# A transformer trunk on one core: where the sums of weight blocks stand, and when weight buffers are returned

## The chip, the core and the metric

The kernel runs on one core of a Trainium2 chip. The core has five engines that run side by side, each with its own stream of instructions: TensorE (PE in the profile; its weight loads are shown as PEld), VectorE (DVE), ScalarE (ACT), GpSimd (POOL) and SyncE (SP), which here only starts DMAs. Weights lie in the chip's main memory and are copied by DMA into on-chip buffers. Matmul results go to eight banks of a separate memory (tiles named `ps`), from which VectorE or ScalarE reads them out; this is called an evacuation below.

The metric is the time of the whole kernel on the device in microseconds (us), a median of runs. Lower is better.

## What is computed

Two requests (512 and 256 tokens, width 1024) go through two layers with shared weights. Each layer is a feed-forward block, a token mixer (a gated linear recurrence in layer 0, windowed attention in layer 1) and a second feed-forward block. The four feed-forward blocks take most of the time, and the change touches only their weights:

```python
def swiglu_ffn(x, w1, w2):
    gate, up = jnp.split(x @ w1, 2, axis=-1)
    return (jax.nn.silu(gate) * up) @ w2

x = x + 0.5 * swiglu_ffn(rmsnorm(x, norm_g[li, 0]), ffn_w1[li, 0], ffn_w2[li, 0])
```

`w1` is 1024 x 5632 and `w2` 2816 x 1024, all in float32.

## The kernel before

**Precision.** TensorE multiplies in a shorter format here (`fp32r`). To keep float32 accuracy each operand is split into a high part (a cast on ScalarE, line 199 for these weights) and a low part (the difference, on VectorE, line 200), and each product is three matmuls: high x high, high x low, low x high.

**Seven products for eight.** The feed-forward products are done as 2 x 2 blocks with a Strassen-like scheme: seven products `p1` to `p7` of sums of blocks replace the eight of the plain scheme. For the weights this means four blocks `a11`, `a12`, `a21`, `a22` and sums of them. They are made in place in the buffers into which the weights were loaded (`wr` in the profile, four of them):

- a DMA that accumulates, started by POOL (`into`, line 141), adds `a22` onto `a21`. This sum is the weight of `p5`;
- another such DMA adds `a11` onto a separately loaded tile `s3`. This is the weight of `p7`;
- `second` (line 205, VectorE) adds `a21` onto `a11`. This is the weight of `p6`;
- `fourth` (line 206, VectorE) adds `a11` onto `a12`. This is the weight of `p3`.

`p1`, `p2` and `p4` take `a11`, `a12` and `a22` as they are; so `second` must come after `a11` was split for `p1` and copied onto `s3`, and `fourth` after `a12` was split for `p2`.

**Two kinds of block.** An *up pair* (`up_pair`, line 424) makes one 128-wide block of `gate` and one of `up` for all tokens: seven products of 12 matmuls over 384 columns (line 414), in the order p1, p7, p2, p5, p4, p6, p3. Its weight blocks are 512 wide and the high and low part of one product share one buffer. Between the products stand the evacuations: lines 431, 433 and 435 on ScalarE, 437, 440, 441, 442, 444, 446 and 448 on VectorE. Line 437 reads the bank of `p5`, on which `p3` then accumulates. A *down block* (`down_quad`) multiplies what four up pairs made by 512 rows of `w2`: seven products of 18 matmuls over 512 columns (line 472), in the order p1, p2, p5, p4, p7, p6, p3, each evacuated by three additions to `x` (line 494). `p2` accumulates on the banks of `p1`, `p4` on those of `p5`, `p3` on those of `p7`. Its weight blocks are 1024 wide, and a product takes two buffers. There are 80 up pairs and 20 down blocks, in groups of four pairs (in a feed-forward's first group two, after other work) and one down block.

After an up pair its two results are split and summed too (lines 259 and 260 for the splits, 343 to 347 for the sums), which gives the operands of the down block.

**Staging.** The split weights live in a ring of eight buffers (`w`). `done` returns the buffers of a product and calls `ahead`, which stages the next products as far as the ring allows; each staging step is one call of `step`, so one product. When all steps of a block have been called, the next block's loads can be issued by SP (line 151; the loads of `s3` are on line 185); they wait until the `wr` buffers they go into have been read for the last time. In `up_pair`, `done` is called at the end of `product`, so ahead of the evacuation that follows it in the code.

**What sets the order.** Each engine runs its instructions in a fixed order, and an instruction that waits holds those behind it on its engine. That order is not the order of the code: the framework places every instruction by its own estimate of when its inputs are there, and where several could go, the one that the code calls first. `issue_after(i)` adds an edge to that: what is traced in it on the engine of instruction `i` is placed behind `i`. It is an order, not a wait for `i` to finish.

Of the kernel before, what the change touches and what calls it, by code (L numbers as in the profile page):

```python
# [9 lines left out]
F32 = mybir.dt.float32  # L10
# [37 lines left out]
class Trunk:  # L48
# [123 lines left out]
    def quad_steps(self, key, raws, srcs, order):  # L172
        nc = self.nc
        flat = lambda t: t.rearrange("p a b -> p (a b)")
        up = len(raws) == 2
        if up:
            a11, a12, a21, a22 = (flat(t[:, h : h + 4, :]) for t in raws for h in (0, 4))
            three = [srcs[1].rearrange("(k p) c -> p k c", p=P)[:, :4, :]]
        else:
            a11, a12, a21, a22 = (flat(t) for t in raws)  # L180
            three = [srcs[2][:, i : i + 1, :] for i in range(2)]
        s3 = []
        for i, src in enumerate(three):
            t = self.wp.tile([P, 512], F32, tag="s3", name=self.name("s3"), bufs=2)
            self.last_load = nc.sync.dma_start(t.rearrange("p (a b) -> p a b", a=src.shape[1]), src)
            self.into(t, a11[:, i * 512 : (i + 1) * 512])
            s3.append(t)
        self.into(a21, a22)

        def split(name, srcs, eng=None):  # L190
            if up:
                w = self.wtile()
                hi, lo = w[:, :512], w[:, 512:]
            else:
                hi, lo = self.wtile(), self.wtile()
            n = srcs[0].shape[-1]
            for i, src in enumerate(srcs):
                h, l = (t[:, i * n : (i + 1) * n] for t in (hi, lo))
                nc.scalar.copy(h, src)  # L199
                (eng or nc.vector).tensor_sub(l, src, h.bitcast(F32))  # L200
            view = lambda t: t.rearrange("p (a b) -> p a b", a=4 if up else 2)
            self.staged[(*key, name)] = (view(hi), view(lo), 1 if up else 2)

        own = {"p1": [a11], "p2": [a12], "p3": [a12], "p4": [a22], "p5": [a21], "p6": [a11], "p7": s3}
        second = lambda: nc.vector.tensor_add(a11, a11, a21)  # L205
        fourth = lambda: nc.vector.tensor_add(a12, a12, a11)  # L206
        after = {"p1": second, "p2": fourth} if up else {"p7": second, "p6": fourth}

        def step(name):
            split(name, own[name], nc.gpsimd if up and name == "p5" else None)  # L210
            if name in after:
                after[name]()

        return [(1 if up else 2, lambda name=name: step(name)) for name in order]

    def stage_next(self):
# [41 lines left out]
    def split(self, src, hi, lo):  # L258
        self.nc.scalar.copy(hi, src)  # L259
        self.nc.vector.tensor_sub(lo, src, hi.bitcast(F32))  # L260
# [148 lines left out]
    def product(self, key, name, src, ps, first, last):  # L409
        wh, wl = self.take((*key, name))  # L410
        for k in range(4):
            a, b = (wh[:, k, :], wl[:, k, :]), self.operand(src, k)
            for i, (x, y) in enumerate(((0, 0), (0, 1), (1, 0))):
                self.nc.tensor.matmul(  # L414
                    ps,
                    a[x],
                    b[y],
                    start=first and k == 0 and i == 0,
                    stop=k == 3 and i == 2,
                    skip_group_check=True,  # L420
                )
        self.done((*key, name))

    def up_pair(self, tag, j):
        nc = self.nc
        key = (tag, j)
        a, b, c, d = (self.ps(H) for _ in range(4))
        v, w, t = (self.tmp(H) for _ in range(3))
        p = lambda name, ps, first, last: self.product(key, name, FACTOR[name], ps, first, last)
        p("p1", a, True, False)  # L430
        nc.scalar.copy(v, a)
        p("p7", c, True, False)
        nc.scalar.copy(w, c)
        p("p2", a, False, True)
        nc.scalar.activation(a, a, AF.Silu)
        p("p5", d, True, False)
        nc.vector.tensor_sub(w, w, d)  # L437
        p("p4", c, False, True)
        p("p6", b, True, True)
        nc.vector.tensor_sub(v, v, b)  # L440
        nc.vector.tensor_sub(t, c, v)
        nc.vector.tensor_mul(t, t, a)  # L442
        yield t
        nc.vector.tensor_sub(w, w, v)
        p("p3", d, False, True)
        nc.vector.tensor_add(v, v, d)
        self.last_act = nc.scalar.activation(v, v, AF.Silu).ins
        self.last_dve = nc.vector.tensor_mul(w, v, w).ins
        yield w

    def down_quad(self, tag, g, hid):
# [823 lines left out]
```

## Time and profile before

| | |
|---|---|
| median of 3 runs | 2866.38 us (2860.94, 2866.38, 2866.47) |
| span of the profiled execution | 2863.4 us |
| mean granted TensorE clock | 0.997 |
| matmuls of up pairs (line 414) | 1174.0 us busy, 6720 |
| matmuls of down blocks (line 472) | 587.2 us busy, 2520 |
| lows of weight splits on VectorE (line 200) | 519.4 us busy, 640 |
| sums on VectorE (lines 205 and 206) | 160.6 us busy, 200 |

The span runs from the first to the last instruction of the profiled execution. The page gives no separate device time for that execution; its span lies within the range of the three runs.

A row such as `1306.90 1.22 DVE L205 ... [6.53 <-DMA wr<-wr]` in a timeline reads: it starts 1306.90 us after the span's start, takes 1.22 us, runs on VectorE, comes from line 205, and the engine was idle for 6.53 us before it, until a DMA into a `wr` buffer landed. In groups, the numbers behind the bar are busy time, mean ns of one, and the idle time of the engine just before them, with what ended it. The matmuls overlap, and their ends are modelled.

### The profile page before, as it was taken

Reading aid. Unit: us, or ns where it says so; the run is one execution under the profiler, and the core shown is the slowest. Engines: PE = TensorE matmul, PEld = TensorE weight load, DVE = VectorE, ACT = ScalarE, POOL = GpSimd, SP = SyncE. Lnnn points to the kernel's source line nnn. Section 1 sums busy time; section 2 is a strip of 40 time slices with the busy share of each in tenths; the row PEclk is TensorE's granted clock in tenths of the full one; section 3 lists DMA queues with packets and bytes.
Section 4 is the critical chain, followed back from the end, with each engine's and each line's share of the span. In section 5 each row is a group of like instructions: output and inputs, shape, how many; then the busy total and the mean of one; then the engine's idle time right before and its main releaser. Section 6 shows DMA issues by size and latency. Waiting matters only on the chain.

```text
span 2863.4 us, 40520 instructions
## 1 busy us (share of the span) xinstructions
PE 2800.4 (98%) x15225; PEld 2556.8 (89%) x15225; DVE 2198.4 (77%) x3846; ACT 1318.5 (46%) x2454; POOL 304.4 (11%) x306
## 2 busy tenths in 40 slices
PE   8999999999999999999999999999999899999998
PEld 8899998889899889988998998999887779988997
DVE  7788788477577658788878877887859978778877
ACT  7344443434344435444445543444457755434443
POOL 1111120000000001111110111111000001111110
PEclk9999999999999999999999999999999999999999
DMA  6555454311111233555444355445412113554443
GB/s 166 126 124 125 116 133 119 109 45 38 52 38 30 74 88 89 133 129 124 118 118 109 88 134 126 121 119 122 126 63 74 45 38 92 132 129 120 120 122 96
DMA packets 330101, 291.37 MB, mean 102 GB/s; under 512 B 11608, under 2 KB 257840, under 8 KB 329904
## 3 DMA queue, kind: packets, MB, share of 16 engines
q1 hardware_dynamic: 294064, 212.43, 25.2%
q0 software_dynamic: 31680, 62.93, 12.5%
q10 hardware_dynamic: 4160, 13.42, 1.3%
q8 instruction: 119, 1.95, 0.3%
q14 instruction: 78, 0.64, 0.1%
HBM read 216.39 MB, written 9.44 MB: 79 GB/s over the span
## 4 chain that ended last, share of the span: by engine, by line
PE 68%; DVE 21%; DMA 5%; issue 3%; ACT 3%; DVEq 0%; ACTq 0%; POOLq 0%; SPq 0%
PE ps L414 24%; PE ps L472 11%; PE ps L254 8%; PE ps L255 8%; PE ps L256 8%; DVE w L200 5%; DVE big L260 3%; PE ps L664 3%; DVE x L494 3%; DMA wr<-wr 3%; DMA wr<-in_ffn_w_dram 3%; DVE tA L347 1%; DVE wr L206 1%; PE ps L758 1%; PE ps L316 1%
## 5 line engine op out<-in xcount | busy, mean ns | idle before, releaser
L414 PE MATMUL ps<-big,w 128*128 128x384 f32 x6720 | 1174.0, 335 | 6.6 <-DVE tA L437 6.2
L414 PEld LDWEIGHTS ps<-big,w 128*128 128x128 f32 x6720 | 1166.0, 188 | 12.7 <-DVE tA L437 11.2
L199 ACT CAST w<-wr 128x512 fp32r<-128x512 f32 x600 | 415.9, 707 | 724.2 <-PE ps L414 317.0
L472 PE MATMUL ps<-w,big 128*128 128x512 f32 x2520 | 587.2, 392 | 17.3 <-DVE x L494 17.3
L472 PEld LDWEIGHTS ps<-w,big 128*128 128x128 f32 x2520 | 470.4, 188 | 129.2 <-DVE x L494 16.6
L200 DVE TENSOR_TENSOR w<-wr,w 128x512 fp32r<-128x512 f32 (+1 forms) x520 | 437.1, 851 | 95.8 <-ACT w L199 87.1
L494 DVE SCALAR_TENSOR_TENSOR x<-ps,x 128x512 f32<-128x512 f32 x468 | 305.9, 683 | 20.4 <-PE ps L472 10.2
L141 POOL DMA_DIRECT2D s<-wr x120 | 105.6, 880 | 1619.8 <-DMA wr<-in_ffn_w_dram 585.7
L254 PE MATMUL ps<-w,big 128*128 128x512 f32 x624 | 248.9, 399 | 0.2
L256 PE MATMUL ps<-w,big 128*128 128x512 f32 x624 | 244.9, 393 | 2.2 <-DVE big L323 1.3
L255 PE MATMUL ps<-w,big 128*128 128x512 f32 x624 | 244.2, 391 | 0.0
L259 ACT CAST big<-tA 128x384 fp32r<-128x384 f32 x296 | 147.9, 513 | 178.9 <-DVE tA L442 77.1
L254 PE MATMUL ps<-big,w 128*128 128x384 f32 (+2 forms) x640 | 220.8, 346 | 3.4 <-ACT big L259 2.0
L255 PE MATMUL ps<-big,w 128*128 128x384 f32 (+2 forms) x640 | 216.9, 339 | 0.7 <-DVE big L260 0.5
L256 PE MATMUL ps<-big,w 128*128 128x384 f32 (+2 forms) x640 | 215.7, 337 | 0.0
L167 DVE TENSOR_TENSOR w<-wr,w 128x1024 fp32r<-128x1024 f32 x92 | 111.4, 1221 | 81.0 <-ACT w L166 56.9
L260 DVE TENSOR_TENSOR big<-tA,big 128x384 fp32r<-128x384 f32 x296 | 167.4, 576 | 8.1 <-ACT big L259 4.9
L205 DVE TENSOR_TENSOR wr<-wr,wr 128x512 f32<-128x512 f32 (+1 forms) x100 | 79.4, 794 | 119.1 <-DMA wr<-wr 89.7
L141 POOL DMA_DIRECT2D wr<-wr x100 | 87.2, 872 | 687.6 <-DVE tA L343 321.4
L166 ACT CAST w<-wr 128x1024 fp32r<-128x1024 f32 x92 | 96.6, 1052 | 120.3 <-PE ps L255 99.4
L256 PEld LDWEIGHTS ps<-w,big 128*128 128x128 f32 x624 | 117.1, 188 | 28.2 <-DVE big L323 2.0
L254 PEld LDWEIGHTS ps<-w,big 128*128 128x128 f32 x624 | 117.4, 188 | 22.4 <-issue 0.6
(170 smaller groups left out, 3296.8 us busy)
## 6 DMA issues: line engine op xcount, KB each, us to landing
wr<-in_ffn_w_dram SPq DMA_DIRECT2D x264, 512.0 KB, 3.9
s<-in_ffn_w_dram SPq DMA_DIRECT2D x120, 256.0 KB, 3.0
s<-wr POOLq DMA_DIRECT2D x120, 256.0 KB, 4.0
wr<-wr POOLq DMA_DIRECT2D x80, 256.0 KB, 3.8
wr<-in_hg_w_in_dram SPq DMA_DIRECT2D x40, 512.0 KB, 3.7
wr<-wr POOLq DMA_DIRECT2D x20, 512.0 KB, 4.6
spill<-x ACTq DMA_DIRECT2D x12, 512.0 KB, 3.1
x<-spill ACTq DMA_DIRECT2D x12, 512.0 KB, 3.3
```

The source lines that it names most:

```text
L141: self.nc.gpsimd.dma_start(out, src, accum_op=ALU.add)
L167: self.nc.vector.tensor_sub(lo, raw, hi.bitcast(F32))
L199: nc.scalar.copy(h, src)
L200: (eng or nc.vector).tensor_sub(l, src, h.bitcast(F32))
L254: nc.tensor.matmul(out, a[0], b[0], start=first, stop=False)
L255: nc.tensor.matmul(out, a[0], b[1], start=False, stop=False)
L256: nc.tensor.matmul(out, a[1], b[0], start=False, stop=last)
L259: self.nc.scalar.copy(hi, src)
L260: self.nc.vector.tensor_sub(lo, src, hi.bitcast(F32))
L414: self.nc.tensor.matmul(ps, a[x], b[y], start=first and k == 0 and i == 0, stop=k == 3 and i == 2, skip_group_check=True,)
L472: nc.tensor.matmul(ps, a[x], w[y], start=name == chain and kp == 0 and q == 0, stop=kp == 1 and q == 2, skip_group_check=True,)
L494: self.nc.vector.scalar_tensor_tensor(x, ps, c, x, ALU.mult, ALU.add)
```

## The change

Each sum moves from behind the split of an earlier product to right in front of the split that reads it. `second` is now part of the step of `p6`, and `fourth` of the step of `p3`, for both kinds of block. Each sum is placed behind the last low part that VectorE made for the same block (for an up pair that of `p4` and that of `p6`; for a down block that of `p7` and that of `p6`).

In `up_pair` the buffers are returned behind the evacuations: those of p1, p7, p2 and p5 after the evacuation next to them, those of p4 and p6 together after line 442 (as numbered before), that of p3 at the very end. `product` no longer returns them. `down_quad` is not touched.

```diff
@@ in quad_steps
             for i, src in enumerate(srcs):
                 h, l = (t[:, i * n : (i + 1) * n] for t in (hi, lo))
                 nc.scalar.copy(h, src)
-                (eng or nc.vector).tensor_sub(l, src, h.bitcast(F32))
+                low = (eng or nc.vector).tensor_sub(l, src, h.bitcast(F32)).ins
             view = lambda t: t.rearrange("p (a b) -> p a b", a=4 if up else 2)
             self.staged[(*key, name)] = (view(hi), view(lo), 1 if up else 2)
+            return low
 
         own = {"p1": [a11], "p2": [a12], "p3": [a12], "p4": [a22], "p5": [a21], "p6": [a11], "p7": s3}
-        second = lambda: nc.vector.tensor_add(a11, a11, a21)
-        fourth = lambda: nc.vector.tensor_add(a12, a12, a11)
-        after = {"p1": second, "p2": fourth} if up else {"p7": second, "p6": fourth}
+        sums = {"p6": (a11, a21), "p3": (a12, a11)}
+        last = [None]
 
         def step(name):
-            split(name, own[name], nc.gpsimd if up and name == "p5" else None)
-            if name in after:
-                after[name]()
+            if name in sums:
+                into, term = sums[name]
+                with self.tc.issue_after(last[0]):
+                    nc.vector.tensor_add(into, into, term)
+            low = split(name, own[name], nc.gpsimd if up and name == "p5" else None)
+            if not (up and name == "p5"):
+                last[0] = low
@@ in product
-        self.done((*key, name))
@@ in up_pair
+        free = lambda *names: [self.done((*key, name)) for name in names]
         p("p1", a, True, False)
         nc.scalar.copy(v, a)
+        free("p1")
         p("p7", c, True, False)
         nc.scalar.copy(w, c)
+        free("p7")
         p("p2", a, False, True)
         nc.scalar.activation(a, a, AF.Silu)
+        free("p2")
         p("p5", d, True, False)
         nc.vector.tensor_sub(w, w, d)
+        free("p5")
         p("p4", c, False, True)
         p("p6", b, True, True)
         nc.vector.tensor_sub(v, v, b)
         nc.vector.tensor_sub(t, c, v)
         nc.vector.tensor_mul(t, t, a)
+        free("p4", "p6")
         yield t
         nc.vector.tensor_sub(w, w, v)
         p("p3", d, False, True)
         nc.vector.tensor_add(v, v, d)
         self.last_act = nc.scalar.activation(v, v, AF.Silu).ins
         self.last_dve = nc.vector.tensor_mul(w, v, w).ins
+        free("p3")
         yield w
```

## The prediction

> **What bounds the kernel now.** I read the page first, then the chain of work that ended last, then the waits and the groups by shape, and last the timeline of one block of the feed-forward part.
>
> ```profile
> span 2863.4 us, 40520 instructions
> PE 2800.4 (98%) x15225; PEld 2556.8 (89%) x15225; DVE 2198.4 (77%) x3846; ACT 1318.5 (46%) x2454; POOL 304.4 (11%) x306
> ```
>
> TensorE is busy for 98% of the span, so any gain has to come out of its gaps. The full pace of its matmuls is read from undisturbed stretches of the chain (start, duration, what):
>
> ```profile
> 54.81 27.06 PE ps L414 x156
> 1237.96 14.80 PE ps L472 x64
> ```
>
> That is 0.173 us for one matmul of an up product (L414) and 0.231 us for one of a down product (L472). Now the waits that reach TensorE in these lines, and one that does not name it (engine, line, releaser: us in total, times, longest):
>
> ```profile
> PE ps L472 <- DVE x L494: 17.3, 37, 0.5
> PE ps L414 <- DVE tA L437: 6.2, 8, 2.3
> PEld ps L414 <- DVE tA L437: 11.2, 15, 2.7
> DVE wr L205 <- DMA wr<-wr: 89.7, 15, 8.2
> ```
>
> L494 and L437 are evacuations on VectorE. L205 is the first of the two sums of weight blocks. By shape it looks like this:
>
> ```profile
> L205 DVE TENSOR_TENSOR wr<-wr,wr 128x1024 f32<-128x1024 f32 x20 | 24.5, 1226 | 118.6 <-DMA wr<-wr 89.7 <-issue 28.9
> L205 DVE TENSOR_TENSOR wr<-wr,wr 128x512 f32<-128x512 f32 x80 | 54.9, 686 | 0.6
> L206 DVE TENSOR_TENSOR wr<-wr,wr 128x1024 f32<-128x1024 f32 x20 | 24.4, 1218 | 0.0
> ```
>
> All of the idle time stands before the 20 sums of the down blocks (1024 wide): 118.6/20 = 5.9 us each. The 80 of the up pairs wait for nothing. So each of the 20 down blocks has one place where VectorE stands still, and I read one of them. TensorE:
>
> ```profile
> 1309.79 2.35 PE L414 MATMUL ps<-big,w 128*128 128x384 f32 x12 [0.83 <-DVE tA L437]
> 1311.97 4.28 PE L472 MATMUL ps<-w,big 128*128 128x512 f32 x18
> 1316.80 10.27 PE L472 MATMUL ps<-w,big 128*128 128x512 f32 x44 [0.55 <-DVE x L494]
> 1327.52 14.80 PE L472 MATMUL ps<-w,big 128*128 128x512 f32 x64 [0.45 <-DVE x L494]
> ```
>
> Three waits: before p3 of the last up pair, before p2 of the down block (it accumulates on p1's bank, which must be read out first), and before p4 (on p5's bank; 44 = 18 of p2, 18 of p5, and 8 of p7 put ahead of p4). A shown gap understates the loss: a matmul is drawn 0.334 us long but follows its neighbour by 0.173, so 0.16 us more are lost at each. VectorE in the same stretch:
>
> ```profile
> 1299.16 1.22 DVE L200 TENSOR_TENSOR w<-wr,w 128x1024 fp32r<-128x1024 f32 x1
> 1306.90 1.22 DVE L205 TENSOR_TENSOR wr<-wr,wr 128x1024 f32<-128x1024 f32 x1 [6.53 <-DMA wr<-wr]
> 1308.05 1.22 DVE L200 TENSOR_TENSOR w<-wr,w 128x1024 fp32r<-128x1024 f32 x1
> 1309.18 0.55 DVE L437 TENSOR_TENSOR tA<-tA,ps 128x384 f32<-128x384 f32 x1
> 1309.64 1.22 DVE L206 TENSOR_TENSOR wr<-wr,wr 128x1024 f32<-128x1024 f32 x1
> 1310.78 1.22 DVE L200 TENSOR_TENSOR w<-wr,w 128x1024 fp32r<-128x1024 f32 x1
> 1311.92 0.55 DVE L440 TENSOR_TENSOR tA<-tA,ps 128x384 f32<-128x384 f32 x1
> 1313.90 1.22 DVE L200 TENSOR_TENSOR w<-wr,w 128x1024 fp32r<-128x1024 f32 x1
> 1315.97 0.68 DVE L494 SCALAR_TENSOR_TENSOR x<-ps,x 128x512 f32<-128x512 f32 x1
> ```
>
> The lows of p1, p2, p5 and p4 are the four L200. In the code the sum L205 is called after p7's split; here it ran second, before p2's low, and held VectorE 6.5 us for the accumulating DMA into a21. L437 waited behind it: product p5 ended some 24 matmuls (4.2 us) and the lost 1.0 us before 1309.79, at 1304.6, and L437 began at 1309.18. Then VectorE works without a gap up to the first L494, 0.7 us too late for p2.
>
> **The change: the sums.** For a down block both sums leave this stretch; L205 must follow p7's low, L206 p6's. No wait on the DMA moves with L205: the cast of p5 reads the same a21 earlier.
>
> ```profile
> 1301.10 1.05 ACT L199 CAST w<-wr 128x1024 fp32r<-128x1024 f32 x1
> 1306.84 1.06 ACT L199 CAST w<-wr 128x1024 fp32r<-128x1024 f32 x1 [3.62 <-DMA wr<-wr]
> ```
>
> These are the casts of p2 and p5. ScalarE still waits for the DMA at p5's, as before; its evacuations of the pair stand ahead of it.
>
> First term, L437. Without the sum, p2's low follows its cast (1302.2 to 1303.4) and L437 runs at 1304.6, when p5 ends. The wait before p3 goes: 6.2 + 8 × 0.16 = 7.5 us, and the seven waits that only the weight loads show (15 less 8) at about 0.15 each, 1 us: **8.5 us**. In one block the wait was so long that more came behind it (timeline of TensorE, then engines in windows, with the granted clock after POOL):
>
> ```profile
> 1723.71 3.14 PE L414 MATMUL ps<-big,w 128*128 128x384 f32 x12 [2.33 <-DVE tA L437]
> 1725.00:1727.00 2.00, 2.00 (x8) 1.98 (x7) 1.97 (x4) 0.00 (x0) 0.00 (x0) 0.51 0.00 1
> 1727.00:1729.00 2.00, 2.00 (x7) 1.54 (x6) 2.00 (x4) 0.51 (x1) 0.00 (x0) 0.64 0.84 244
> ```
>
> Clocks of 0.51 and 0.64 over 2 us each lose 1.0 + 0.7 = **1.7 us**, which go with the wait. The Trainium skill, "TensorE: Matmul & The Clock Gate", section "Part 1: The HAM clock gate", has the clock fall after an idle window of about 3.4 us; by that a gap of 2.33 us would not cause it, and the sum would be smaller by this term. Here it fell behind a shorter gap, so I keep the term.
>
> Second term, p2. p5's low now ends at 1307.9 + 1.15 = 1309.05. Behind it, at the paces of the rows (start to start), come L440 to L442 (1313.90 − 1311.92 = 1.98) and p4's low, L260 and L446 (1315.97 − 1313.90 = 2.07): the first L494 starts at 1313.1 and ends at 1313.8. TensorE, 1.0 us earlier, begins p1 at 1311.0 and wants p2 at 1311.0 + 18 × 0.231 = 1315.1: 1.3 us of cover. All 37 waits come to 17.3 + 37 × 0.16 = 23.2 us; divided as 0.71 to 0.61 that is **12.5 us** for p2's, which go, and 10.7 us for p4's. In the block of 1723.71 the DMA came 1.5 us later, and some of p2's wait stays there.
>
> Third term, p4. Before, 10.81 us pass from the first L494 to p5's, and p6's low is in them:
>
> ```profile
> 1322.74 0.69 DVE L200 TENSOR_TENSOR w<-s,w 128x512 fp32r<-128x512 f32 x1
> 1325.64 1.22 DVE L200 TENSOR_TENSOR w<-wr,w 128x1024 fp32r<-128x1024 f32 x1
> 1326.78 1.88 DVE L494 SCALAR_TENSOR_TENSOR x<-ps,x 128x512 f32<-128x512 f32 x3
> 1321.88 1.05 ACT L199 CAST w<-wr 128x1024 fp32r<-128x1024 f32 x1
> ```
>
> The sum (1.15 us) now stands behind p7's last low (1322.74), and p6's cast (1321.88) must wait for it; p6's low should then fall behind p5's evacuation. One goes in and one out: p5's first L494 starts at 1313.1 + 10.8 = 1323.9 and ends at 1324.6. p4 is wanted at 1311.0 + 54 × 0.231 = 1323.5, or 8 matmuls later (1325.3) if p7's still stand ahead. So the wait is between 0 and 1.1 us, against 0.61: from 10.7 us gained to 20 × 0.5 = 10 us lost. I take two thirds of the gain, **7 us**, since the order with the 8 matmuls is the one in the trace. p6's and p3's weights come some 3 us later (sum, cast 1.05, low 1.14 twice), at 1331 at the latest; p6 begins at 1311.0 + 90 × 0.231 = 1331.8 and p3 four us on. Cover of 1 us at the least; beyond it the cost is one for one.
>
> **What is held longer.** L205 reads a21, so a21's raw buffer comes free after it, no longer after p5's low. SP loads the next pair's weights into that buffer:
>
> ```profile
> 1312.03 3.49 SPq L151 DMA_DIRECT2D wr<-in_ffn_w_dram  x2
> 1331.74 0.62 ACT L199 CAST w<-wr 128x512 fp32r<-128x512 f32 x1 [5.62 <-PE ps L472]
> wr<-in_ffn_w_dram SPq DMA_DIRECT2D x264, 512.0 KB, 3.9
> s<-in_ffn_w_dram SPq DMA_DIRECT2D x120, 256.0 KB, 3.0
> s<-wr POOLq DMA_DIRECT2D x120, 256.0 KB, 4.0
> ```
>
> The load went out at 1312.03, as p5's low ended (1310.78 + 1.22). It will go out at 1321 to 1324, and the second load, the s3 load and POOL's two accumulations queue behind it: 3.9, then 3.0 and 4.0 with under 2 us of issuing, so p7's s3 stands at 1337 at the latest. Its split takes 1.3 us more; TensorE wants that at 1327.52 + 14.80, less the 2.3 us gained in this block, plus p1's 2.1: 1342.1. Hidden with some 4 us; ScalarE and VectorE may stand 2 to 3 us at p7's split, which I put at **2 us lost** in all. L206 holds a11's buffer in the same way, for a load wanted a pair later.
>
> **Up pairs.** 160 sums move by four products and cost the same 0.69 us. a21's buffer comes free 0.7 us later, against a lead of some 8 products (8 × 12 × 0.173 = 16.6 us). Nothing.
>
> **Returning buffers behind the evacuations.** It adds no instruction. The cast no longer stands ahead of L431, L433, L435: those come 0.5 us sooner, the cast as much later. No wait of TensorE names these three, so nothing is gained, and 0.5 us is covered by the same 16.6 us. p4's buffer comes back with p6's, some 4 us later; still covered, and costing nothing until the lead is gone.
>
> **Sum.** 8.5 + 1.7 + 12.5 + 7 − 2 = 27.7 us, from a span of 2863.4 to 2835.7. The runs shown have a median of 2866.38, 3.0 us above this span (they reach from 2860.94 to 2866.47, so this profiled execution is an ordinary one). Against the median: 2838.7, say **2839 us**.
>
> **Rivals.**
>
> *Only the L437 wait goes.* The gaps before p2 and p4 are alike in nearly every block, 0.55 and 0.45, although L205 waited between 5 and 8.2 us. That speaks for a cause that does not hang on the sum: too few banks, or the evacuation being simply wanted at once. Against it: VectorE is without a gap for 9 us before the first L494, and 3.5 us of that leave. It gives 8.5 + 1.7 = 10 us: 2856. The Trainium skill, "Perfetto Trace Analysis", section "Optimization Strategy", reads a repeating gap on the saturated engine as a possible lack of SBUF or PSUM for the next tile; by that, this rival is the right one. In these rows the releaser of each gap is an evacuation, which fits either reading.
>
> *The order does not follow.* The edges bind only VectorE's sums; everything else is ordered by the scheduler's own estimate, which put L205 where the DMA was not done. It can do the same with another instruction (p5's low ahead of L437 would bring back a wait of 1307.9 + 1.2 − 1304.6 − 4.2, about 0.3 us in a block, and p2's with it), or p4's term turns to 10 us lost. Gains and losses within 6 us: 2862 to 2870, centre 2866.
>
> *Slower: the late buffer starves the next pair.* The place is p7 of the first pair after each of 20 down blocks; the point is L205 ending about 4 us later than my 1324. Two more puts and three more evacuations ahead of it would do that, as p7's lows are already drawn apart by them. 2.5 us beyond the point at 20 places is 50 us, less the 30 us gained above: 2886. For it: the load's start moves by 9 to 12 us. Against it: the 4 us left.
>
> **How the numbers follow.** My forecast 0.57 (its own range 2829 to 2850), only L437 0.18, no follow-through 0.12, starved pair 0.13. Faster by over 0.2% (5.7 us, about what a measurement of this kernel can tell from no change): 0.57 + 0.18 = 0.75; within it 0.12; slower 0.13. The range leaves out the starved pair and a little below the forecast: 2828 to 2868.
>
> **What would show it.** Right: L205 of 1024 elements no longer has a DMA as releaser, stands behind p7's second low, and its 118.6 us of idle time are gone; PE L414 has no wait on L437; the L472 waits on L494 fall from 37 to under 15; no clock under 1 near the down blocks. Wrong: waits of L472 on L494 as many as before (second rival); waits of L414 on a cast or low of L199/L200 behind the down blocks (the starved pair); or VectorE idle before an L200 with a DMA or L199 as releaser while L437 is due.

## The result, and the profile after

The changed kernel takes 2833.75 us (median of 4 runs, 2833.56 to 2837.87) against 2866.28 us before: a ratio of 0.9897, 95% interval 0.9884 to 0.9910, so 32.5 us or 1.1% faster. The forecast was 2839 us. The profiled execution took 2833.56 us; its span is 31.6 us shorter than before:

```profile
span 2831.8 us, 40534 instructions
PE 2790.5 (99%) x15225; PEld 2559.2 (90%) x15225; DVE 2203.1 (78%) x3846; ACT 1320.2 (47%) x2453; POOL 307.3 (11%) x306
PE 91%; DVE 6%; ACT 2%; issue 1%; DMA 0%; DVEq 0%; ACTq 0%; SPq 0%
```

The third line is the chain of work that ended last. Before, TensorE held 68% of it, VectorE 21% and DMAs 5%; now TensorE holds 91%.

Line numbers have moved: up matmuls are L418 (were L414), down matmuls L482 (L472), both sums L213 (L205, L206), the evacuations of a down block L504 (L494), of p5 in an up pair L444 (L437), the copy of p1's bank L435 (L431). In the groups by shape (two rows of the kernel before, then the changed kernel), and then in the waits of the changed kernel:

```profile
L414 PE MATMUL ps<-big,w 128*128 128x384 f32 x6720 | 1174.0, 335 | 6.6 <-DVE tA L437 6.2
L472 PE MATMUL ps<-w,big 128*128 128x512 f32 x2520 | 587.2, 392 | 17.3 <-DVE x L494 17.3
```

```profile
L418 PE MATMUL ps<-big,w 128*128 128x384 f32 x6720 | 1173.8, 335 | 1.5 <-ACT tA L435 1.4
L482 PE MATMUL ps<-w,big 128*128 128x512 f32 x2520 | 576.6, 390 | 0.7 <-DVE x L504 0.6
L213 DVE TENSOR_TENSOR wr<-wr,wr 128x1024 f32<-128x1024 f32 x40 | 48.6, 1215 | 0.0
```

```profile
PEld ps L418 <- ACT tA L435: 6.4, 19, 0.8
PE ps L482 <- DVE x L504: 0.6, 1, 0.6
ACT w L199 <- DVE wr L213: 342.8, 132, 4.9
```

Busy plus idle time tells where the gain is. Before, the down matmuls had 587.2 + 17.3 = 604.5 us, now 576.6 + 0.7 = 577.3: 27.2 us gained. The up matmuls had 1174.0 + 6.6 = 1180.6, now 1175.3: 5.3 us. Together 32.5, which is the whole difference of the spans but for 0.9 us lost elsewhere. The 118.6 us for which VectorE stood before the wide sums are gone. Of the waits on L494 one is left, of 37; there is none on L444. One is new: TensorE's weight loads wait for the copy L435, and behind it is the third line: ScalarE now waits 342.8 us in all for sums of VectorE.

A down block of the changed kernel has no gap (timeline of TensorE, then of VectorE):

```profile
1304.59 28.92 PE L482 MATMUL ps<-w,big 128*128 128x512 f32 x126
```

```profile
1298.55 0.56 DVE L444 TENSOR_TENSOR tA<-tA,ps 128x384 f32<-128x384 f32 x1 [0.45 <-PE ps L418]
1302.08 1.23 DVE L200 TENSOR_TENSOR w<-wr,w 128x1024 fp32r<-128x1024 f32 x1 [2.98 <-ACT w L199]
...
1307.74 0.68 DVE L504 SCALAR_TENSOR_TENSOR x<-ps,x 128x512 f32<-128x512 f32 x1
...
1316.83 1.22 DVE L213 TENSOR_TENSOR wr<-wr,wr 128x1024 f32<-128x1024 f32 x1
...
1320.96 1.21 DVE L213 TENSOR_TENSOR wr<-wr,wr 128x1024 f32<-128x1024 f32 x1
```

```profile
1300.99 1.05 ACT L199 CAST w<-wr 128x1024 fp32r<-128x1024 f32 x1 [4.06 <-DMA wr<-wr]
```

L444, the evacuation of p5, runs as soon as p5 ends. The last row is ScalarE's cast of p5, which waits for the DMA; VectorE waits for that cast at p5's low (1302.08). The sums come 12 and 16 us after p1's start. But the cover before p2 is thin: p2 is due at 1304.59 + 18 × 0.231 = 1308.75, and p1's first evacuation ends at 1308.42.

### The profile page after: what moved, and what is told of

Same layout as the page of the kernel before. It is cut to its first block, busy times and chain, and to the rows that moved or that the text cites. A ratio compares the mean times of both kernels' runs of the same rounds, so it can differ in the third digit from the quotient of the medians.

```text
span 2831.8 us, 40534 instructions
## 1 busy us (share of the span) xinstructions
PE 2790.5 (99%) x15225; PEld 2559.2 (90%) x15225; DVE 2203.1 (78%) x3846; ACT 1320.2 (47%) x2453; POOL 307.3 (11%) x306
## 4 chain that ended last, share of the span: by engine, by line
PE 91%; DVE 6%; ACT 2%; issue 1%; DMA 0%; DVEq 0%; ACTq 0%; SPq 0%
PE ps L418 38%; PE ps L482 20%; PE ps L259 8%; PE ps L258 8%; PE ps L260 8%; PE ps L674 3%; PE ps L768 1%; DVE w L200 1%; DVE big L264 1%; PE ps L320 1%; PE ps L1147 1%; PE ps L744 1%; DVE w L167 0%; PE ps L1109 0%; DVE big L1112 0%
## 5 line engine op out<-in xcount | busy, mean ns | idle before, releaser
L418 PE MATMUL ps<-big,w 128*128 128x384 f32 x6720 | 1173.8, 335 | 1.5 <-ACT tA L435 1.4
L418 PEld LDWEIGHTS ps<-big,w 128*128 128x128 f32 x6720 | 1165.2, 188 | 8.4 <-ACT tA L435 6.4
L199 ACT CAST w<-wr 128x512 fp32r<-128x512 f32 x600 | 416.1, 707 | 689.2 <-DVE wr L213 342.8
L200 DVE TENSOR_TENSOR w<-wr,w 128x512 fp32r<-128x512 f32 (+1 forms) x520 | 447.8, 865 | 185.8 <-ACT w L199 174.8
L482 PE MATMUL ps<-w,big 128*128 128x512 f32 x2520 | 576.6, 390 | 0.7 <-DVE x L504 0.6
L482 PEld LDWEIGHTS ps<-w,big 128*128 128x128 f32 x2520 | 472.1, 188 | 100.1 <-ACT big L263 1.5
L504 DVE SCALAR_TENSOR_TENSOR x<-ps,x 128x512 f32<-128x512 f32 x468 | 304.3, 683 | 10.8 <-PE ps L260 10.0
L263 ACT CAST big<-tA 128x384 fp32r<-128x384 f32 x296 | 148.0, 513 | 151.5 <-DVE tA L450 70.3
L264 DVE TENSOR_TENSOR big<-tA,big 128x384 fp32r<-128x384 f32 x296 | 180.3, 620 | 12.9 <-ACT big L263 12.0
L260 PEld LDWEIGHTS ps<-w,big 128*128 128x128 f32 x624 | 117.1, 188 | 28.0 <-DVE big L987 1.7
L200 POOL TENSOR_TENSOR w<-wr,w 128x512 fp32r<-128x512 f32 x80 | 123.8, 1547 | 166.9 <-ACT w L199 146.9
L259 PEld LDWEIGHTS ps<-w,big 128*128 128x128 f32 x624 | 117.4, 188 | 22.3
L258 PEld LDWEIGHTS ps<-w,big 128*128 128x128 f32 x624 | 117.3, 188 | 22.2 <-issue 0.3
```

Source lines behind the costliest of these rows:

```text
L200: low = (eng or nc.vector).tensor_sub(l, src, h.bitcast(F32)).ins
L258: nc.tensor.matmul(out, a[0], b[0], start=first, stop=False)
L259: nc.tensor.matmul(out, a[0], b[1], start=False, stop=False)
L260: nc.tensor.matmul(out, a[1], b[0], start=False, stop=last)
L418: self.nc.tensor.matmul(ps, a[x], b[y], start=first and k == 0 and i == 0, stop=k == 3 and i == 2, skip_group_check=True,)
L482: nc.tensor.matmul(ps, a[x], w[y], start=name == chain and kp == 0 and q == 0, stop=kp == 1 and q == 2, skip_group_check=True,)
```

## The experiments

Two theories stood at the start. **Theory Q**: the early sum of a down block holds VectorE until its DMA has landed, and what is queued behind it comes late. **Rival R**: the returns behind the evacuations made the evacuations early. **Rival U** is that the 80 up pairs' sums count too. All runs are in this table; "up" and "down" are busy plus idle time of their matmuls in the profiled execution, and "first wide sum" is VectorE's idle time before the first sum of the down blocks. The kernel before took 2862.3 to 2863.1 us on the chips of the later runs.

| run | median, us | ratio to before, 95% interval | up, us | down, us | first wide sum, us |
|---|---|---|---|---|---|
| before | 2866.28 | | 1180.6 | 604.5 | 118.6 |
| changed | 2833.75 | 0.9897, 0.9884 to 0.9910 | 1175.3 | 577.3 | 0.0 |
| sums_only | 2833.12 | 0.9893, 0.9878 to 0.9908 | 1172.8 | 577.1 | 0.0 |
| returns_only | 2859.38 | 0.9984, 0.9975 to 0.9994 | 1177.1 | 602.9 | 117.1 |
| late_down | 2866.31 | 1.0008, 0.9994 to 1.0022 | 1169.1 | 610.7 | 0.0 |
| late_up | 2867.76 | 1.0015, 1.0006 to 1.0024 | 1180.5 | 604.0 | 68.1 |
| no_edges | 2860.30 | 0.9988, 0.9978 to 0.9997 | 1175.1 | 602.8 | 114.9 |
| behind_p5 | 2852.65 | 0.9965, 0.9951 to 0.9979 | 1175.2 | 594.5 | 0.0 |
| fourth_late | 2837.24 | 0.9913, 0.9898 to 0.9928 | 1175.3 | 582.1 | 112.2 |
| late_first | 2825.91 | 0.9873, 0.9858 to 0.9888 | 1169.2 | 575.3 | 0.0 |
| changed_again | 2834.84 | 0.9902, 0.9887 to 0.9917 | 1174.5 | 577.6 | 0.0 |
| late_first_again | 2827.20 | 0.9876, 0.9859 to 0.9892 | 1169.2 | 575.3 | 0.0 |
| late_first_old_returns | 2826.91 | 0.9874, 0.9860 to 0.9889 | 1169.2 | 575.3 | 0.0 |

### One part alone: sums, or returns

`sums_only` is the change without its part in `product` and `up_pair`; `returns_only` is that part alone.

```diff
 sums_only, against the changed kernel
+        self.done((*key, name))          # at the end of product, as before
...
-        free("p1")                       # and the other four calls in up_pair
 returns_only, against the changed kernel
-        sums = {"p6": (a11, a21), "p3": (a12, a11)}
...
+        after = {"p1": second, "p2": fourth} if up else {"p7": second, "p6": fourth}
```

> Only the sums are moved; up pairs return their buffers as before. Theory Q (the early sum of a down block holds VectorE until its DMA has landed, and what is queued behind it is late): all of the gain is here, 2832 to 2838 us, no wait of the down matmuls on their evacuations. Rival R (the evacuations were late because staging stood ahead of them, and the returns cured it): 2855 us or more, with p2's and p4's waits still there.

> Only the returns are moved; the sums stand where they did. Theory Q: within 4 us of 2866, with the 20 sums of the down blocks still idle some 6 us each until the DMA. Rival R: 2840 us or less.

Measured: 0.9893 with the sums alone, which is the whole gain; 0.9984 with the returns alone. Rival R falls. The returns are not quite nothing by themselves (the interval ends at 0.9994; the waits on p5's evacuation fall from 6.2 us to the 3.9 us below), but on top of the sums they add nothing that can be measured.

```profile
PE ps L415 <- DVE tA L441: 3.9, 8, 1.5
```

### Half of the sums: down blocks alone, or up pairs alone

```diff
 in quad_steps, against the changed kernel
+        late = not up                    # late_down;  late_up: late = up
 ...
-        sums = {"p6": (a11, a21), "p3": (a12, a11)}
+        after = {} if late else {"p1": second, "p2": fourth} if up else {"p7": second, "p6": fourth}
+        sums = {"p6": (a11, a21), "p3": (a12, a11)} if late else {}
```

> The changed kernel, but up pairs make their sums early again; only the 20 down blocks have theirs late. Theory Q: the gain of the down blocks stays whole, and ScalarE's casts no longer wait for late sums in the up pairs, so the wait before p2 of the last pair of a group (6.4 us of weight loads behind the copy of p1's bank) goes too: 2828 to 2833 us. Rival U (the up pairs' sums in their dense stretch mattered as well): 2838 us or more.

> The other half: only the 80 up pairs have their sums late, the down blocks have them early. Theory Q: no gain, 2864 to 2870 us, the 118 us of idle time before the 1024-wide sum still there. Rival U: 2858 us or less.

`late_up` gains nothing, as expected (it is 0.15% slower, just clear of the noise). One thing in it was not expected: the idle time before the first wide sum falls from 118.6 to 68.1 us, and still nothing is gained. The surprise is the other run. `late_down`, which has everything that theory Q asks for, gains nothing either (1.0008). Its waits before p2 and p4 are gone; in their place stand longer ones before p3, the last product of the down block (waits, and the timelines of TensorE and VectorE in the block with the longest wait):

```profile
PE ps L492 <- DVE x L514: 25.5, 17, 3.1
DVE wr L206 <- issue: 60.7, 20, 4.8
```

```profile
1320.63 14.90 PE L492 MATMUL ps<-w,big 128*128 128x512 f32 x65
1338.59 5.92 PE L492 MATMUL ps<-w,big 128*128 128x512 f32 x18 [3.06 <-DVE x L514]
```

```profile
1331.62 0.69 DVE L200 TENSOR_TENSOR w<-s,w 128x512 fp32r<-128x512 f32 x1
1337.15 0.69 DVE L206 TENSOR_TENSOR wr<-wr,wr 128x512 f32<-128x512 f32 x1 [4.85 <-issue]
1337.76 1.88 DVE L514 SCALAR_TENSOR_TENSOR x<-ps,x 128x512 f32<-128x512 f32 x3
```

L206 is here the early sum of the next *up pair*. It holds VectorE for 60.7/20 = 3.0 us in each block, and p7's evacuations, for whose banks p3 waits, stand behind it. The profile calls the releaser "issue", but ScalarE's row for the same moment names it: the cast of the same pair's p5 starts as the accumulating DMA lands.

```profile
1337.22 1.66 ACT L199 CAST w<-wr 128x512 fp32r<-128x512 f32 x3 [5.34 <-DMA wr<-wr]
```

The DMA is late because its load is: POOL could start it only when the load had landed (first row below, `late_down`). A late sum keeps a21's buffer, and the next pair's second load goes into it. In the changed kernel, too, that load leaves only when the sum has ended (1316.83 + 1.22 = 1318.05; the other two rows):

```profile
1330.12 0.86 POOL L141 DMA_DIRECT2D wr<-wr  x1 [5.65 <-DMA wr<-in_ffn_w_dram]
```

```profile
1306.92 0.37 SPq L151 DMA_DIRECT2D wr<-in_ffn_w_dram  x1
1318.07 6.97 SPq L151 DMA_DIRECT2D wr<-in_ffn_w_dram  x3
```

The two loads leave 2.3 and 13.5 us after p1's start at 1304.59; before, the two loads left 0.1 and 3.2 us after it (1312.03 and 1315.15, the first start of a row of two and its end less 0.37, with p1 at 1311.97). So the same kind of hold moves from the down block's sum to the next pair's, unless that one is late as well. The changed kernel does both, and no wait of TensorE is left there. Part of the price in `late_down` is the clock: behind three of the waits the 18 matmuls of p3 took 5.92 to 5.97 us (in the one above at a granted clock of 0.50), behind the others 4.33 to 4.37.

### Is the place in the code enough?

```diff
 against the changed kernel
-                with self.tc.issue_after(last[0]):
+                with nullcontext():
                     nc.vector.tensor_add(into, into, term)
```

> The changed kernel without the order edges: the sums are only called later. Theory Q: the down blocks' first sum is placed ahead of p2's low again and waits there for its DMA some 6 us; the gain is gone for the most part, 2855 to 2866 us. Rival (the place in the code is enough): 2832 to 2836 us.

Measured 0.9988, and 114.9 us of idle time before the first wide sum: without the edge the framework places the sum where it was. What is left, 0.12%, is about what the returns gave alone.

### The hold, or the work in the way?

Theory Q has two terms that come together in the change: VectorE stands still, and 2.3 us of sums lie ahead of p1's evacuations. `behind_p5` takes away the first and leaves the second (its first sum still follows the same DMA, since it stands behind p5's low); `fourth_late` takes away only half of the second.

```diff
 behind_p5, against the changed kernel, down blocks only
-        sums = {"p6": (a11, a21), "p3": (a12, a11)}
+        after = {"p5": second, "p4": fourth}      # each with issue_after(last[0])
 ...
 fourth_late, against the kernel before, down blocks only
-        after = {"p7": second, "p6": fourth}
+        after = {"p7": second}
+        sums = {"p3": (a12, a11)}                 # fourth, with issue_after(last[0])
 ...
```

> The changed kernel with the down blocks' sums early but never the first to wait: the first sum right behind p5's low (whose cast has waited for the same DMA), the second behind p4's low, both ahead of the first evacuation of the down block. This tells the held VectorE from the work that stands ahead of the evacuations. If the hold alone cost the time: 2832 to 2838 us. If the work counts as well (in the changed kernel p1's first evacuation ends only 0.26 us before p2 wants the bank, and 2.3 us are put ahead of it): waits of 1 to 2 us before p2 in the 20 blocks, none behind L437's place, 2854 to 2874 us.

> The kernel before with one thing changed: the second sum of the down blocks stands behind p6's low; the first stays early and holds VectorE. Theory Q with both terms: the waits before p3 of the last pair stay (8 to 10 us in all), the waits before p2 go (1.14 us less work against 0.7 us of lateness), so 2840 to 2853 us. If the hold alone cost the time: within 4 us of before.

With the sums early but never waiting, two thirds of the gain are lost: 0.9965, just under the range that the work term gave. There is no wait on p5's evacuation, and each of the 20 blocks waits at its second product:

```profile
PE ps L489 <- DVE x L511: 12.7, 20, 1.2
```

```profile
1309.95 5.64 PE L489 MATMUL ps<-w,big 128*128 128x512 f32 x24
1316.32 23.47 PE L489 MATMUL ps<-w,big 128*128 128x512 f32 x102 [0.73 <-DVE x L511]
```

```profile
1308.32 1.22 DVE L206 TENSOR_TENSOR wr<-wr,wr 128x1024 f32<-128x1024 f32 x1
...
1313.98 1.22 DVE L207 TENSOR_TENSOR wr<-wr,wr 128x1024 f32<-128x1024 f32 x1
1315.12 0.55 DVE L271 TENSOR_TENSOR big<-tA,big 128x384 fp32r<-128x384 f32 x1
1315.59 0.68 DVE L511 SCALAR_TENSOR_TENSOR x<-ps,x 128x512 f32<-128x512 f32 x1
```

p2 was due at 1309.95 + 4.16 = 1314.11 and its bank was free at 1316.27, 2.2 us late. The expectation's 1 to 2 us of waiting was too high only because the framework had put six matmuls of a later product (24 − 18, 1.4 us) ahead of p2, so 0.73 us is shown as a wait.

`fourth_late` is the mirror image: one instruction of a block is moved, and VectorE is still held for 112.2 us in all. The ratio is 0.9913, four fifths of the change's gain. The first two rows are the waits on p5's evacuation in the up pair, which were expected to stay. The third stands before p4 of the down block, where now only the weight loads show it:

```profile
PE ps L425 <- DVE tA L448: 2.9, 6, 1.3
PEld ps L425 <- DVE tA L448: 6.4, 12, 1.6
PEld ps L483 <- DVE x L505: 8.8, 17, 0.6
```

None is before p2, and the down matmuls take 582.1 us against 604.5. Curing the hold alone gives a third of the gain, and less work alone four fifths. The shares add to more than one: a wait that is 0.7 us long is cured by either, once it frees that much, so the two cannot be split into parts of a sum. What the runs do show is that the work that the sums put into a stretch with no slack counted for more than VectorE's standing still. `late_up` agrees: 50 us of idle time went there, with both sums still ahead of the evacuations, and nothing was gained. The expected 2840 to 2853 us was too slow by 3 us: p4's wait went for the most part too. Whether an earlier landing of the DMA would have done the same was not tried.

### A version with both holds cured

The changed kernel still loses some time at the copy L435. In one block (the timelines of ScalarE, VectorE and TensorE):

```profile
1956.51 1.58 ACT L199 CAST w<-wr 128x512 fp32r<-128x512 f32 x2 [1.44 <-DVE wr L213]
1958.55 0.51 ACT L263 CAST big<-tA 128x384 fp32r<-128x384 f32 x1 [0.46 <-DVE tA L450]
1959.68 0.53 ACT L456 ACTIVATE tA<-tA 128x384 f32<-128x384 f32 x1 [0.62 <-DVE tA L455]
1960.11 0.46 ACT L435 COPY tA<-ps 128x384 f32<-128x384 f32 x1
```

```profile
1955.10 0.69 DVE L200 TENSOR_TENSOR w<-wr,w 128x512 fp32r<-128x512 f32 x1 [0.76 <-ACT w L199]
1955.71 0.69 DVE L213 TENSOR_TENSOR wr<-wr 128x512 f32<-128x512 f32 x1
```

```profile
1960.62 4.61 PE L418 MATMUL ps<-big,w 128*128 128x384 f32 x25 [0.30 <-ACT tA L435]
```

ScalarE's casts wait for late sums, and VectorE's lows for those casts. The evacuations behind them on VectorE come late, and so do the cast L263 and the activation L456, which wait for two of them (L450, L455); the copy stands right behind these. By the finding on `late_down`, only the pair behind a down block needs its sums late; the other 60 could have them early. (Each feed-forward block ends with two pairs behind its last down block; the first of them is such a pair too.)

```diff
 against the changed kernel
+        late = not up or key[1] % 4 == 0
 ...
-        sums = {"p6": (a11, a21), "p3": (a12, a11)}
+        after = {} if late else {"p1": second, "p2": fourth}
+        sums = {"p6": (a11, a21), "p3": (a12, a11)} if late else {}
```

> Late sums in the 20 down blocks and in the one up pair that follows each of them, early sums in the other 60 pairs. Theory Q with the finding that a late sum in the down block delays the next pair's load, whose early sum then holds VectorE: that place is cured and ScalarE's casts wait less for sums, 2826 to 2833 us. Rival (all pairs have to be late): 2845 us or more, with waits before p3 of the down blocks.

> The changed kernel itself, beside the two below on one chip: 2831 to 2838 us.

> Late sums in the down blocks and in the pair behind each: 6 to 9 us less than the changed kernel, 2824 to 2830 us, with no wait of the up or down matmuls on VectorE or ScalarE. Rival (the difference of the earlier runs was the chip's): within 3 us of the changed kernel.

> The same sums, but up pairs return their buffers where they did before the change. If the returns hide nothing that is left: within 2.5 us of late_first_again. If they are what keeps ScalarE's copies ahead of the casts that wait for sums: 3 to 8 us slower, with a wait of the up matmuls on the copy of p1's bank.

Side by side on one chip: 2834.84 us for the changed kernel, 2827.20 and 2826.91 us with early sums in the 60 pairs, 7.6 us or 0.27% less. The ranges of the single runs do not touch (2833.45 to 2835.94, 2826.08 to 2828.73, 2825.00 to 2828.73), though the intervals of their ratios to before overlap a little. Where the returns stand makes no difference that can be measured. In the profile of `late_first_again`, both kinds of matmul have no idle time at all:

```profile
L426 PE MATMUL ps<-big,w 128*128 128x384 f32 x6720 | 1169.2, 334 | 0.0
L490 PE MATMUL ps<-w,big 128*128 128x512 f32 x2520 | 575.3, 389 | 0.0
```

These are the fastest kernels run, at 0.9873 to 0.9876 of the time before in the three runs of the table.

## Why the prediction held, and where it was wrong

- **The bound.** Right: the gaps of TensorE in the feed-forward blocks were the whole gain, 32.5 us of busy plus idle time.
- **First term, L437.** The wait went as said. But of 8.5 us the up matmuls kept 5.3, since waits on the copy L435 (L431 before) came in its place. Without any wait they take 1169.2 us (`late_first`), so before they had lost 11.4 us, and in the changed kernel they lose 6.1. The forecast said that no wait of TensorE names L431, L433 or L435, and took them for safe; that the moved sums would make VectorE and ScalarE late ahead of the copy was not seen.
- **The clock, 1.7 us.** The slow stretch behind the long wait is gone, and its cost with it: it is in the two gains, with 0.8 us in the up matmuls (3.14 us for the 12 at 1723.71, where others took 2.35) and 0.9 us in the down block behind them. But the changed kernel has a slow stretch elsewhere, in the first token mixer, where the kernel before has none, and one instead of two in the second (near 2224, where the kernel before has them near 2248 and 2258); the mean clock is 0.997 in both. Two profiles can't tell whether the whole gained anything by it.

```profile
1723.00:1727.00 4.00, 4.00 (x19) 3.02 (x18) 3.73 (x5) 1.05 (x1) 0.40 (x1) 1.00 0.67 149
581.80:585.00 3.20, 3.20 (x17) 3.20 (x16) 2.10 (x4) 0.92 (x1) 0.00 (x0) 0.50 0.00 0
```

- **Second and third term, p2 and p4.** The mechanism was right, the size of the third was not: 12.5 + 7 = 19.5 us were forecast, 27.2 measured. p4's wait went whole, not by two thirds. And a wait cost more than gap plus 0.16: in the block with gaps of 0.55 and 0.45 us, 30.18 us pass from p1's start to the next pair's (1311.97 to 1342.15), but 28.60 where nothing waits (1300.63 to 1329.23 in `late_first_again`). That is 1.58 us for two waits, not 1.32, or some 0.13 us more for each of the 37; why was not tried. The cover before p2 was forecast as 1.3 us and is 0.3. About 0.6 us of that is the DMA, which lands later against TensorE than before: p5's cast waits until 3.6 us before p1 starts, against the 4.2 that the forecast took (1311.0 − 1306.84). Another 0.5 us is L457 (L448 before), which now stands ahead of the first L504 on VectorE and stood behind it before. In one block, where the DMA is later still, 0.61 us are left, as the forecast said of it.
- **The held buffer.** The delay of the load into a21's buffer was about right: it leaves 13.5 us after p1's start, where the forecast had 10 to 13 (1321 to 1324, with p1 at 1311.0). But this is now only the second of the pair's two loads; the first took a22's buffer, which comes free as before. The 2 us that the forecast lost at p7's split are not found: no wait of the up matmuls stands in the first pair behind a down block. The waits on L435 have another cause, the late sums of the up pairs.
- **The up pairs: "Nothing".** This is the step that failed. The forecast gave the move of their 160 sums no part in the result, but without it the change is worth nothing: `late_down` takes 2866.31 us. (The move of 40 of them, in the 20 pairs behind down blocks, is enough, and the other 120 cost more than they give: `late_first`.) The forecast had the starved pair as its slower rival and followed its weights to TensorE, where they had 4 us of cover; it did not ask which instruction on VectorE would wait for the late DMA. With early sums in the pairs that is the pair's own sum, and the price is some 32 us (2866.31 − 2833.75), two thirds of the 50 at which the rival was priced. The change moves that sum too, and so escapes it; that the forecast came out right here was luck.
- **The sum.** 31.6 us came off the span where 27.7 were forecast. Some of that nearness is luck: the up matmuls gave 4 us less than their terms with the clock's 0.8, the down matmuls 7 us more than theirs with its 0.9, the loss of 2 us did not come, and 0.9 us were lost elsewhere.
- **The rivals.** "Only the L437 wait goes" is shown wrong: the gaps before p2 and p4 were VectorE's lateness, and follow the work ahead of them (`behind_p5`, `fourth_late`). With the same eight banks and buffers they are gone, so the reading as a lack of memory falls too. "The order does not follow" did not come either; `no_edges` shows that it takes the edges to make the order follow.

## What to carry to other kernels

An instruction that is not urgent does harm in two ways where an engine has no slack: by waiting, and by its own length. Here its length counted for more, and moving one 1.2 us sum per block gave four fifths of the gain. When an instruction is moved later, follow the buffer that it holds: what loads into it, which instruction on a busy engine waits for that load, and what is queued behind it. A wait that has been cured in one block can come back in the next one as the same kind of wait.

## What the runs showed of the hardware that was not expected

The clock fell behind some gaps of TensorE and not behind others of the same length. The stretch at 581.80 above follows a gap of 1.74 us. The kernel before has the same gap at the same place, and its clock stays full (the timelines of TensorE in the changed kernel and before, then a window before):

```profile
580.90 2.62 PE L674 MATMUL ps<-big,big 128*128 128x128 f32 x12 [1.74 <-ACT big L699]
```

```profile
585.80 2.25 PE L664 MATMUL ps<-big,big 128*128 128x128 f32 x12 [1.74 <-ACT big L689]
586.00:588.00 2.00, 2.00 (x13) 2.00 (x13) 1.38 (x3) 0.00 (x0) 0.00 (x0) 1.00 0.00 0
```

In `late_down` a gap of 3.06 us (1338.59, above) is followed by a clock of 0.50, and one of 2.23 us by a full clock (TensorE's timeline, then windows). Behind a gap of 2.71 us (at 2712.76) the clock stays full too, and behind one of 2.31 us (at 2802.22) it falls.

```profile
1748.83 4.37 PE L492 MATMUL ps<-w,big 128*128 128x512 f32 x18 [2.23 <-DVE x L514]
```

```profile
1339.00:1342.00 3.00, 3.00 (x9) 2.33 (x8) 3.00 (x7) 0.00 (x0) 1.03 (x2) 0.50 0.52 91
1749.00:1752.00 3.00, 3.00 (x14) 2.44 (x14) 3.00 (x6) 0.12 (x1) 1.29 (x2) 1.00 0.44 78
```

So the length of a gap alone does not tell whether the clock will fall; what else decides was not tried.

VectorE's subtraction of 512 elements takes 0.68 us, but took 1.37 us beside a subtraction of POOL (VectorE, then POOL, in the changed kernel):

```profile
1328.16 0.68 DVE L200 TENSOR_TENSOR w<-wr,w 128x512 fp32r<-128x512 f32 x1
1332.10 1.37 DVE L200 TENSOR_TENSOR w<-wr,w 128x512 fp32r<-128x512 f32 x1 [1.46 <-ACT w L199]
```

```profile
1331.63 1.29 POOL L200 TENSOR_TENSOR w<-wr,w 128x512 fp32r<-128x512 f32 x1 [3.54 <-ACT w L199]
```

VectorE's row ends 0.55 us after POOL's. The Trainium skill, "SBUF — State Buffer", section "SBUF: two separate sides", has a VectorE operation with two inputs in SBUF and a POOL operation that reads SBUF wait for each other whole, which these rows agree with. In the kernel before, a VectorE subtraction that began 0.28 us ahead of POOL's (1335.54 and 1335.82) took 2.46 us, and POOL's 1.62 us, so there both were longer. It was not tried by itself.
